# FiLM scale and shift on one core: small inputs first in 4 KB runs, accumulated matmuls, compute in program order

## The chip, the cores and the metric

One core of a Trainium2 chip runs the whole program. The metric is the device time of one execution in microseconds (us). A run is called slow when it takes over 1.5% more than the fastest of the same kernel; comparisons use the fast runs alone. Ratios compare the fast runs of two kernels in the same rounds, so they are not quite the ratio of the medians quoted. The span is the time that the profile covers; it is about 1.75 us shorter than the measured time.

## The reference

```python
# x [32, 512, 256], conditioning [32, 64], gamma_proj and beta_proj [64, 256], all float32
gamma = conditioning @ gamma_proj
beta = conditioning @ beta_proj
return (x * (1 + gamma[:, None, :]) + beta[:, None, :]).astype(np.float32)
```

Of the data, x comes in (16.78 MB) and the result goes out (16.78 MB). The three small inputs together are 0.14 MB.

## The kernel before

The batch is cut into four slabs of 8 samples; in a slab each of the 128 partitions holds 32 rows of 256 numbers. SyncE's queue loads x, ScalarE's queue loads the small inputs and later stores the result. TensorE makes gamma and beta for a slab, spread over the partitions. VectorE handles 11 of every 16 rows, straight from PSUM, and GpSimd handles the other 5, from a copy that ScalarE makes.

```python
nc.scalar.dma_start(out=cond_s, in_=conditioning)
gbproj = consts.tile([cond_dim, 2 * dim], f32)               # 64 partitions
nc.scalar.dma_start(out=gbproj[:, :dim], in_=gamma_proj)     # 1 KB runs
nc.scalar.dma_start(out=gbproj[:, dim:], in_=beta_proj)
# ... x: slab 0 in pieces of 8 and 24 rows, slabs 1 to 3 whole, all on nc.sync ...
nc.tensor.matmul(cond_T_p, lhsT=cond_s, rhs=rident, start=True, stop=True)
# ... copied to cond_T, then for each slab s:
nc.tensor.matmul(p_t, lhsT=cond_T[:, s * P : (s + 1) * P], rhs=gbproj, start=True, stop=True)
nc.scalar.activation(out=s_t[:, :dim], in_=p_t[:, :dim], ..., bias=1.0, scale=1.0)
nc.scalar.copy(out=s_t[:, dim:], in_=p_t[:, dim:])
# ... and for each half slab of 16 rows: v = 11 rows, w = 5 rows
nc.vector.scalar_tensor_tensor(out=v, in0=rows(g_p, nv), scalar=1.0, in1=v, op0=ALU.add, op1=ALU.mult)
nc.gpsimd.tensor_tensor(out=w, in0=w, in1=rows(g_s, nw), op=ALU.mult)
nc.vector.tensor_add(out=v, in0=v, in1=rows(b_p, nv))
nc.gpsimd.tensor_tensor(out=w, in0=w, in1=rows(b_s, nw), op=ALU.add)
nc.scalar.dma_start(out=o_v[s, :, r0 : r0 + GROUP, :], in_=xs[:, r0 : r0 + GROUP, :])
```

Of the kernel before, what the change touches and what calls it, by code (L numbers as in the profile page):

```python
# [2 lines left out]

# [5 lines left out]


@with_exitstack
def kernel(
    ctx: ExitStack,
    tc: tile.TileContext,
    x: bass.AP,
    conditioning: bass.AP,
    gamma_proj: bass.AP,
    beta_proj: bass.AP,
    out: bass.AP,  # L20
):
    nc = tc.nc
    f32 = mybir.dt.float32
    ALU = mybir.AluOpType

    batch, seq, dim = x.shape
    cond_dim = conditioning.shape[1]
    P = 128
    SLABS = 4
    BS = batch // SLABS  # L30
    REP = P // BS
    ROWS = BS * seq // P
    assert SLABS * BS == batch and REP * BS == P and ROWS * REP == seq

    x_v = x.flatten_outer_dims().rearrange("(s p r) d -> s p r d", s=SLABS, p=P)
    o_v = out.flatten_outer_dims().rearrange("(s p r) d -> s p r d", s=SLABS, p=P)

    LOADS = {0: [8, 24]}
    GROUP = 16
    ON_DVE = 11  # L40

    consts = ctx.enter_context(tc.tile_pool(name="consts", bufs=1))
    xpool = ctx.enter_context(tc.tile_pool(name="xpool", bufs=1))
    psum = ctx.enter_context(tc.tile_pool(name="psum", bufs=1, space=bass.MemoryType.PSUM))


    cond_s = consts.tile([batch, cond_dim], f32)
    nc.scalar.dma_start(out=cond_s, in_=conditioning)  # L48
    gbproj = consts.tile([cond_dim, 2 * dim], f32)
    nc.scalar.dma_start(out=gbproj[:, :dim], in_=gamma_proj)  # L50
    nc.scalar.dma_start(out=gbproj[:, dim:], in_=beta_proj)

    slabs = []
    for s in range(SLABS):
        xs = xpool.tile([P, ROWS, dim], f32, name=f"xs{s}")
        slabs.append(xs)
        r = 0
        for n in LOADS.get(s, [ROWS]):
            nc.sync.dma_start(out=xs[:, r : r + n, :], in_=x_v[s, :, r : r + n, :])
            r += n  # L60
        assert r == ROWS


    ident = consts.tile([batch, batch], f32)
    make_identity(nc, ident)
    rident = consts.tile([batch, batch * REP], f32)
    nc.vector.tensor_copy(  # L67
        out=rident.rearrange("p (b g) -> p b g", g=REP),
        in_=ident.to_broadcast([batch, batch, REP]),
    )  # L70
    cond_T_p = psum.tile([cond_dim, batch * REP], f32)
    nc.tensor.matmul(cond_T_p, lhsT=cond_s, rhs=rident, start=True, stop=True)  # L72
    cond_T = consts.tile([cond_dim, batch * REP], f32)
    nc.vector.tensor_copy(out=cond_T, in_=cond_T_p)  # L74

    gb_p, gb_s = [], []
    for s in range(SLABS):
        p_t = psum.tile([P, 2 * dim], f32, name=f"gb_p{s}")
        nc.tensor.matmul(p_t, lhsT=cond_T[:, s * P : (s + 1) * P], rhs=gbproj,  # L79
                         start=True, stop=True)  # L80
        s_t = consts.tile([P, 2 * dim], f32, name=f"gb_s{s}")
        nc.scalar.activation(out=s_t[:, :dim], in_=p_t[:, :dim],  # L82
                             func=mybir.ActivationFunctionType.Identity,
                             bias=1.0, scale=1.0)
        nc.scalar.copy(out=s_t[:, dim:], in_=p_t[:, dim:])  # L85
        gb_p.append(p_t)
        gb_s.append(s_t)

    def rows(t, n):
        return bass.AP(tensor=t.tensor, offset=t.offset, ap=[t.ap[0], [0, n], t.ap[1]])  # L90

    for s in range(SLABS):
        xs = slabs[s]
        g_p, b_p = gb_p[s][:, :dim], gb_p[s][:, dim:]
        g_s, b_s = gb_s[s][:, :dim], gb_s[s][:, dim:]
        for r0 in range(0, ROWS, GROUP):
            v = xs[:, r0 : r0 + ON_DVE, :]
            w = xs[:, r0 + ON_DVE : r0 + GROUP, :]
            nv, nw = ON_DVE, GROUP - ON_DVE
            nc.vector.scalar_tensor_tensor(out=v, in0=rows(g_p, nv), scalar=1.0, in1=v,  # L100
                                           op0=ALU.add, op1=ALU.mult)
            nc.gpsimd.tensor_tensor(out=w, in0=w, in1=rows(g_s, nw), op=ALU.mult)  # L102
            nc.vector.tensor_add(out=v, in0=v, in1=rows(b_p, nv))  # L103
            nc.gpsimd.tensor_tensor(out=w, in0=w, in1=rows(b_s, nw), op=ALU.add)  # L104
            nc.scalar.dma_start(out=o_v[s, :, r0 : r0 + GROUP, :],
                                in_=xs[:, r0 : r0 + GROUP, :])


# [1 line left out]
_INS = ['x', 'conditioning', 'gamma_proj', 'beta_proj']  # L110
_OUTS = [((32, 512, 256), 'float32')]


# [23 lines left out]
```

## Time and profile before

| | before |
|---|---|
| time, first three runs | 84.39, 85.98, 85.95 us (median 85.95, on which the prediction was made) |
| time, with three more runs beside the changed kernel | median 84.53 us, 84.39 to 85.98 (the four fast runs: 84.39 to 84.54) |
| span of the profiled run | 82.6 us |
| bytes moved | 33.69 MB |
| VectorE's first and last work on x | starts at 17.52, ends at 66.58 us |

### The profile page before, as it was taken

To read this page: it belongs to the slowest core of one execution; us is meant where nothing else is said; L and a number is where in the kernel's file an instruction comes from. 1 tells how busy PE (TensorE), PEld (TensorE's weight loads), DVE (VectorE), ACT (ScalarE), POOL (GpSimd) and SP (SyncE) were. 2 spreads that over 40 slices of the span, in tenths; PEclk is the share of its full clock that TensorE was granted. 3 is DMA by queue.
4 is the path that set the end of the run, shared out by engine and by line. 5 is a ranking of instruction groups with operands and counts; after the bars stand their busy time and mean duration, and the time that the engine had idled before them with its cause. 6 is when DMAs were issued, how large, how long until landed. Compare 5 with 4: busy or idle time off the path is not lost.

```text
span 82.6 us, 156 instructions
## 1 busy us (share of the span) xinstructions
PE 9.1 (11%) x10; PEld 2.8 (3%) x10; DVE 49.9 (60%) x18; ACT 3.9 (5%) x9; POOL 46.2 (56%) x22
## 2 busy tenths in 40 slices
PE   0080000899600000000000000000000000000000
PEld 0100000443000000000000000000000000000000
DVE  2011000059999999999999999999999920000000
ACT  0600000034400000000000000000000000000000
POOL 2000000069999999999999999999995000000000
DMA  3899999969969989998889979899999999999992
GB/s 56 337 508 397 389 397 524 460 302 508 508 270 492 508 381 381 413 476 381 381 381 556 460 302 460 381 468 421 429 452 389 468 421 421 460 389 452 437 421 87
DMA packets 2080, 33.69 MB, mean 408 GB/s; under 512 B 288, under 2 KB 416, under 8 KB 416
## 3 DMA queue, kind: packets, MB, share of 16 engines
q1 hardware_dynamic: 720, 16.78, 48.6%
q10 hardware_dynamic: 1360, 16.92, 48.0%
HBM read 16.92 MB, written 16.78 MB: 408 GB/s over the span
## 4 chain that ended last, share of the span: by engine, by line
DVE 49%; DMA 16%; issue 11%; PE 2%; ACTq 1%; ACT 1%
DVE xs L100 30%; DVE xs L103 19%; DMA gbproj<-in_beta_proj_dram 16%; PE gb_p L79 2%; ACTq L50 1%; ACTq L48 0%; ACT gb_s L82 0%; ACT gb_s L85 0%
## 5 line engine op out<-in xcount | busy, mean ns | idle before, releaser
L102 POOL TENSOR_TENSOR xs<-xs,gb_s 128x1280 f32<-128x1280 f32 x8 | 23.0, 2895 | 16.2 <-ACT gb_s L82 16.2
L100 DVE SCALAR_TENSOR_TENSOR xs<-gb_p,xs 128x2816 f32<-128x2816 f32 x8 | 24.7, 3083 | 10.9 <-ACT gb_s L85 10.9
L103 DVE TENSOR_TENSOR xs<-xs,gb_p 128x2816 f32<-128x2816 f32 x8 | 24.7, 3086 | 0.3
L104 POOL TENSOR_TENSOR xs<-xs,gb_s 128x1280 f32<-128x1280 f32 x8 | 23.0, 2893 | 0.0
L79 PE MATMUL gb_p<-gbproj,cond_T 64*128 64x512 f32 x8 | 7.2, 1074 | 8.9 <-DMA gbproj<-in_beta_proj_dram 8.9
L74 DVE COPY cond_T<-cond_T_p 64x512 f32<-64x512 f32 x1 | 0.7, 683 | 4.3 <-PE cond_T_p L72 4.3
L79 PEld LDWEIGHTS gb_p<-gbproj,cond_T 64*128 64x128 f32 x8 | 2.5, 328 | 13.7 <-issue 13.7
L72 PE MATMUL cond_T_p<-rident,cond_s 32*64 32x512 f32 x2 | 1.9, 1065 | 3.9 <-DMA cond_s<-in_conditioning_dram 3.9
L82 ACT ACTIVATE gb_s<-gb_p 128x256 f32<-128x256 f32 x4 | 1.5, 383 | 16.4 <-PE gb_p L79 16.4
L85 ACT COPY gb_s<-gb_p 128x256 f32<-128x256 f32 x4 | 1.5, 367 | 0.0
L82 ACT ACT_TABLE_LOAD x1 | 1.3, 1283 | 2.4 <-issue 2.4
L67 DVE COPY rident<-ident 32x512 f32<-32x512 f32 x1 | 0.4, 416 | 1.2 <-POOL ident masks.py:199 1.2
L72 PEld LDWEIGHTS cond_T_p<-rident,cond_s 32*64 32x64 f32 x2 | 0.3, 202 | 3.9 <-issue 3.9
masks.py:197 POOL MEMSET ident<- 32x32 f32 x1 | 0.1, 114 | 0.3 <-POOLq L121 0.3
masks.py:199 POOL TENSOR_SCALAR_AFFINE_SELECT ident<-ident 32x32 f32<-32x32 f32 x1 | 0.2, 202 | 0.1
L121 POOL MEMSET const-float32-0.0<- 128x1 f32 x1 | 0.1, 103 | 0.2 <-issue 0.2
L121 POOL MEMSET const-bfloat16-1.0<- 128x1 bf16 x1 | 0.1, 106 | 0.0
L121 POOL MEMSET const-uint8-127<- 128x1 uint8 x1 | 0.1, 106 | 0.0
L121 POOL MEMSET const-float32-1.0<- 128x1 f32 x1 | 0.1, 103 | 0.0
## 6 DMA issues: line engine op xcount, KB each, us to landing
out_dram<-xs ACTq DMA_DIRECT2D x8, 2048.0 KB, 18.2
xs<-in_x_dram SPq DMA_DIRECT2D x3, 4096.0 KB, 32.9
xs<-in_x_dram SPq DMA_DIRECT2D x1, 3072.0 KB, 12.2
xs<-in_x_dram SPq DMA_DIRECT2D x1, 1024.0 KB, 4.6
gbproj<-in_gamma_proj_dram ACTq DMA_DIRECT2D x1, 64.0 KB, 9.1
gbproj<-in_beta_proj_dram ACTq DMA_DIRECT2D x1, 64.0 KB, 12.9
cond_s<-in_conditioning_dram ACTq DMA_DIRECT2D x1, 8.0 KB, 3.0
```

What stands on the lines that cost most here:

```text
L50: nc.scalar.dma_start(out=gbproj[:, :dim], in_=gamma_proj)
L67: nc.vector.tensor_copy(out=rident.rearrange("p (b g) -> p b g", g=REP), in_=ident.to_broadcast([batch, batch, REP]),)
L72: nc.tensor.matmul(cond_T_p, lhsT=cond_s, rhs=rident, start=True, stop=True)
L74: nc.vector.tensor_copy(out=cond_T, in_=cond_T_p)
L79: nc.tensor.matmul(p_t, lhsT=cond_T[:, s * P : (s + 1) * P], rhs=gbproj, start=True, stop=True)
L82: nc.scalar.activation(out=s_t[:, :dim], in_=p_t[:, :dim], func=mybir.ActivationFunctionType.Identity, bias=1.0, scale=1.0)
L85: nc.scalar.copy(out=s_t[:, dim:], in_=p_t[:, dim:])
L100: nc.vector.scalar_tensor_tensor(out=v, in0=rows(g_p, nv), scalar=1.0, in1=v, op0=ALU.add, op1=ALU.mult)
L102: nc.gpsimd.tensor_tensor(out=w, in0=w, in1=rows(g_s, nw), op=ALU.mult)
L103: nc.vector.tensor_add(out=v, in0=v, in1=rows(b_p, nv))
L104: nc.gpsimd.tensor_tensor(out=w, in0=w, in1=rows(b_s, nw), op=ALU.add)
L121: nc = _bacc.Bacc("TRN2", target_bir_lowering=False, num_devices=1)
```

## The change

The intent is to start compute earlier. The projections come as 4 KB runs on 16 partitions, each as the first DMA of its queue, so that they land ahead of x. Sixteen partitions hold four rows each of the 64, so a product becomes four accumulated matmuls. The vector work is put in program order.

```diff
+    CP = 16
+    CJ = cond_dim // CP
     cond_s = consts.tile([batch, cond_dim], f32)
+    gproj = consts.tile([CP, CJ, dim], f32)
+    bproj = consts.tile([CP, CJ, dim], f32)
+    gproj_src = gamma_proj.rearrange("(q j) d -> q j d", j=CJ)
+    bproj_src = beta_proj.rearrange("(q j) d -> q j d", j=CJ)
+    nc.sync.dma_start(out=gproj, in_=gproj_src)
+    nc.scalar.dma_start(out=bproj, in_=bproj_src)
+    load(nc.sync, 0, 0)
     nc.scalar.dma_start(out=cond_s, in_=conditioning)
-    gbproj = consts.tile([cond_dim, 2 * dim], f32)
-    nc.scalar.dma_start(out=gbproj[:, :dim], in_=gamma_proj)
-    nc.scalar.dma_start(out=gbproj[:, dim:], in_=beta_proj)
+    load(nc.sync, 0, 1)
+    # ... slabs 1, 2, 3 on nc.sync
...
-        nc.tensor.matmul(p_t, lhsT=cond_T[:, s * P : (s + 1) * P], rhs=gbproj,
-                         start=True, stop=True)
+        # c_t: this slab's 8 columns of the transposed conditioning, spread over 128
+        for half, proj in ((p_t[:, :dim], gproj), (p_t[:, dim:], bproj)):
+            for j in range(CJ):
+                nc.tensor.matmul(half, lhsT=c_t[:, j, :], rhs=proj[:, j, :],
+                                 start=j == 0, stop=j == CJ - 1)
...
+    with tc.manual_schedule():        # the loop over slabs: instructions as written
```

More of the change, by code (lines that the diff above doesn't have):

```diff
@@ L28 @@
     P = 128
-    SLABS = 4
-    BS = batch // SLABS
-    REP = P // BS
-    ROWS = BS * seq // P
-    assert SLABS * BS == batch and REP * BS == P and ROWS * REP == seq
-    x_v = x.flatten_outer_dims().rearrange("(s p r) d -> s p r d", s=SLABS, p=P)
-    o_v = out.flatten_outer_dims().rearrange("(s p r) d -> s p r d", s=SLABS, p=P)
-    LOADS = {0: [8, 24]}
-    GROUP = 16
-    ON_DVE = 11
+    SLABS = [(8, [8, 24]), (8, [32]), (8, [32]), (8, [32])]
+    assert sum(n for n, _ in SLABS) == batch
+    STORES = [[16, 16], [16, 16], [16, 16], [16, 16]]
+    PIECE, ON_DVE = 16, 11
+    x_f = x.flatten_outer_dims()
+    o_f = out.flatten_outer_dims()
     consts = ctx.enter_context(tc.tile_pool(name="consts", bufs=1))
@@ L44 @@
     psum = ctx.enter_context(tc.tile_pool(name="psum", bufs=1, space=bass.MemoryType.PSUM))
-    cond_s = consts.tile([batch, cond_dim], f32)
-    nc.scalar.dma_start(out=cond_s, in_=conditioning)
-    gbproj = consts.tile([cond_dim, 2 * dim], f32)
-    nc.scalar.dma_start(out=gbproj[:, :dim], in_=gamma_proj)
-    nc.scalar.dma_start(out=gbproj[:, dim:], in_=beta_proj)
-    slabs = []
-    for s in range(SLABS):
-        xs = xpool.tile([P, ROWS, dim], f32, name=f"xs{s}")
-        slabs.append(xs)
-        r = 0
-        for n in LOADS.get(s, [ROWS]):
-            nc.sync.dma_start(out=xs[:, r : r + n, :], in_=x_v[s, :, r : r + n, :])
-            r += n
-        assert r == ROWS
+    slabs = []
@@ new lines, with load @@
+    b0 = 0
+    for s, (n, loads) in enumerate(SLABS):
+        assert P % n == 0
+        rows = n * seq // P
+        r0, r1 = b0 * seq, (b0 + n) * seq
+        slabs.append(dict(
+            n=n, b0=b0, rows=rows, loads=loads,
+            src=x_f[r0:r1, :].rearrange("(p r) d -> p r d", p=P),
+            dst=o_f[r0:r1, :].rearrange("(p r) d -> p r d", p=P),
+            xs=xpool.tile([P, rows, dim], f32, name=f"xs{s}"),
+        ))
+        b0 += n
+    def load(eng, s, i):
+        sl = slabs[s]
+        r = sum(sl["loads"][:i])
+        n = sl["loads"][i]
+        eng.dma_start(out=sl["xs"][:, r : r + n, :], in_=sl["src"][:, r : r + n, :])
@@ L64 @@
+    load(nc.sync, 1, 0)
+    load(nc.sync, 2, 0)
+    load(nc.sync, 3, 0)
     ident = consts.tile([batch, batch], f32)
     make_identity(nc, ident)
-    rident = consts.tile([batch, batch * REP], f32)
-    nc.vector.tensor_copy(
-        out=rident.rearrange("p (b g) -> p b g", g=REP),
-        in_=ident.to_broadcast([batch, batch, REP]),
-    )
-    cond_T_p = psum.tile([cond_dim, batch * REP], f32)
-    nc.tensor.matmul(cond_T_p, lhsT=cond_s, rhs=rident, start=True, stop=True)
-    cond_T = consts.tile([cond_dim, batch * REP], f32)
@@ L74 @@
-    nc.vector.tensor_copy(out=cond_T, in_=cond_T_p)
-    gb_p, gb_s = [], []
-    for s in range(SLABS):
+    gb_p, gb_s = [], []
+    cond_T_p = psum.tile([CP, CJ, batch], f32)
+    for j in range(CJ):
+        nc.tensor.matmul(cond_T_p[:, j, :],
+                         lhsT=cond_s.rearrange("b (q j) -> b j q", j=CJ)[:, j, :],
+                         rhs=ident, start=True, stop=True)
+    for s, sl in enumerate(slabs):
+        n, b0 = sl["n"], sl["b0"]
+        rep = P // n
+        c_t = consts.tile([CP, CJ, P], f32, name=f"cond_T{s}")
+        nc.vector.tensor_copy(
+            out=c_t.rearrange("q j (b g) -> q j b g", g=rep),
+            in_=cond_T_p[:, :, b0 : b0 + n].to_broadcast([CP, CJ, n, rep]),
+        )
@@ L78 @@
         p_t = psum.tile([P, 2 * dim], f32, name=f"gb_p{s}")
-        nc.tensor.matmul(p_t, lhsT=cond_T[:, s * P : (s + 1) * P], rhs=gbproj,
-                         start=True, stop=True)
+        for half, proj in ((p_t[:, :dim], gproj), (p_t[:, dim:], bproj)):
+            for j in range(CJ):
+                nc.tensor.matmul(half, lhsT=c_t[:, j, :], rhs=proj[:, j, :],
+                                 start=j == 0, stop=j == CJ - 1)
         s_t = consts.tile([P, 2 * dim], f32, name=f"gb_s{s}")
@@ L87, with spread @@
         gb_s.append(s_t)
-    def rows(t, n):
+    def spread(t, n):
         return bass.AP(tensor=t.tensor, offset=t.offset, ap=[t.ap[0], [0, n], t.ap[1]])
-    for s in range(SLABS):
-        xs = slabs[s]
-        g_p, b_p = gb_p[s][:, :dim], gb_p[s][:, dim:]
-        g_s, b_s = gb_s[s][:, :dim], gb_s[s][:, dim:]
-        for r0 in range(0, ROWS, GROUP):
-            v = xs[:, r0 : r0 + ON_DVE, :]
-            w = xs[:, r0 + ON_DVE : r0 + GROUP, :]
-            nv, nw = ON_DVE, GROUP - ON_DVE
-            nc.vector.scalar_tensor_tensor(out=v, in0=rows(g_p, nv), scalar=1.0, in1=v,
-                                           op0=ALU.add, op1=ALU.mult)
-            nc.gpsimd.tensor_tensor(out=w, in0=w, in1=rows(g_s, nw), op=ALU.mult)
-            nc.vector.tensor_add(out=v, in0=v, in1=rows(b_p, nv))
-            nc.gpsimd.tensor_tensor(out=w, in0=w, in1=rows(b_s, nw), op=ALU.add)
-            nc.scalar.dma_start(out=o_v[s, :, r0 : r0 + GROUP, :],
-                                in_=xs[:, r0 : r0 + GROUP, :])
+    with tc.manual_schedule():
+        for s, sl in enumerate(slabs):
+            xs = sl["xs"]
+            g_p, b_p = gb_p[s][:, :dim], gb_p[s][:, dim:]
+            g_s, b_s = gb_s[s][:, :dim], gb_s[s][:, dim:]
+            done = 0
+            for n in STORES[s]:
+                for q0 in range(done, done + n, PIECE):
+                    nv, nw = ON_DVE, PIECE - ON_DVE
+                    v = xs[:, q0 : q0 + nv, :]
+                    w = xs[:, q0 + nv : q0 + PIECE, :]
+                    nc.vector.scalar_tensor_tensor(out=v, in0=spread(g_p, nv), scalar=1.0, in1=v,
+                                                   op0=ALU.add, op1=ALU.mult)
+                    nc.gpsimd.tensor_tensor(out=w, in0=w, in1=spread(g_s, nw), op=ALU.mult)
+                    nc.vector.tensor_add(out=v, in0=v, in1=spread(b_p, nv))
+                    nc.gpsimd.tensor_tensor(out=w, in0=w, in1=spread(b_s, nw), op=ALU.add)
+                nc.scalar.dma_start(out=sl["dst"][:, done : done + n, :],
+                                    in_=xs[:, done : done + n, :])
+                done += n
+            assert done == sl["rows"]
 _INS = ['x', 'conditioning', 'gamma_proj', 'beta_proj']
```

## The prediction

> **What bounds the kernel now.** I read the page from the top, then the chain, then the table of stretches, and only then single instructions. First the slices of the span and the queues:
>
> ```profile
> DMA  3899999969969989998889979899999999999992
> ...
> DMA packets 2080, 33.69 MB, mean 408 GB/s; under 512 B 288, under 2 KB 416, under 8 KB 416
> ...
> q1 hardware_dynamic: 720, 16.78, 48.6%
> q10 hardware_dynamic: 1360, 16.92, 48.0%
> ```
>
> The reader is to see that the two queues add up to 96.6% of what the 16 DMA engines can give in 82.6 us. q1 holds the loads of x (16.78 MB), q10 the stores and the three small inputs. VectorE is busy for 60% and GpSimd for 56%. So the transfers are the first candidate, and there is 3.4% of the span, 2.8 us, in which the DMA engines do nothing.
>
> The chain that ended last seems to say something else:
>
> ```profile
> 1.72 12.90 DMA gbproj<-in_beta_proj_dram
> 14.62 0.14 issue
> 14.76 2.06 PE gb_p L79 x2
> ...
> 17.52 3.10 DVE xs L100
> ...
> 63.49 3.09 DVE xs L103
> ```
>
> It runs from the beta projection, which takes 12.9 us to land, over two matmuls and ScalarE to VectorE, which then never stops until 66.58. This is what the change attacks. But the chain follows instructions, and the last of them ends 16 us before the span does. Those 16 us, and what stands before them, are in the table by stretches (start:end, length, five engines, granted clock, DMA share, GB/s):
>
> ```profile
> 2.00:4.00 2.00, 0.08 (x1) 0.11 (x2) 0.00 (x0) 1.28 (x1) 0.00 (x0) 1.00 0.84 324
> 4.00:14.00 10.00, 1.85 (x2) 0.18 (x2) 0.68 (x1) 0.00 (x0) 0.00 (x0) 1.00 1.05 433
> 14.00:26.00 12.00, 7.16 (x8) 2.50 (x8) 8.45 (x3) 2.59 (x8) 8.70 (x4) 1.00 0.98 423
> ...
> 66.00:74.00 8.00, 0.00 (x0) 0.00 (x0) 0.58 (x1) 0.00 (x0) 0.00 (x0) 1.00 1.02 436
> 74.00:80.00 6.00, 0.00 (x0) 0.00 (x0) 0.00 (x0) 0.00 (x0) 0.00 (x0) 1.00 0.99 426
> 80.00:81.00 1.00, 0.00 (x0) 0.00 (x0) 0.00 (x0) 0.00 (x0) 0.00 (x0) 1.00 0.88 377
> ```
>
> From 4 to 80 us the share stays at 0.97 to 1.05 in every stretch, whether only loads run (433 and 423 GB/s), loads and stores mixed (414 to 451), or stores alone (436). While the projections are late, the loads of x use the time; after the last vector instruction a backlog of stores drains. The late start of compute is a wait that the DMA engines do not feel. My reading: the span is about 2 us to get going, 33.69 MB at about 427 GB/s (78.9 us), and 1.6 us after the last data. That sums to 82.5.
>
> **What the Trainium skill says.** (1) "DMA: Bandwidth & Descriptors", section "Where 436 GB/s comes from", gives 435 GB/s as the ceiling of the 16 engines. The trace agrees: 426 to 436 GB/s over the long stretches. (2) The same page, "Queues, rings and completion order", says that each engine takes turns between its queues packet by packet. The trace agrees: 64 KB of gamma took 9.1 us from issue to landing and beta 12.9, while x moved beside them. A projection of 64 rows gives each engine four 1 KB packets, each of which waits for a packet of x (8 KB, then 24 KB). (3) The same page, "Why a DMA increments its semaphore by 16 and not by 1", says that the slowest dimension sets how many engines a DMA uses, up to 16. Sixteen partitions should thus still use all 16, with one 4 KB packet each. The trace before has no 16-partition DMA to show it. (4) "TensorE: Matmul & The Clock Gate", "Step-by-step: what each phase is for", says that weights can be loaded behind a running matmul, and that the load's time goes by columns, not rows. The trace agrees on the first: loads of 334 ns started every 0.85 us, with no gap in the matmuls.
>
> **The change part by part.** *Small inputs.* Gamma goes first on SyncE's queue and beta first on ScalarE's, as 32 packets of 4 KB in place of 128 of 1 KB. Nothing long stands ahead of them; 128 KB at 427 GB/s is 0.3 us, so both should land by about 3.5 us (the 8 KB conditioning, first in line before, landed at 3.7). Conditioning is now second and issued 0.5 us later, with two packets per engine that take turns with 8 KB packets of x (about 0.3 us each): landing at about 4.5. The first x issue slips by the 0.4 us of gamma's issue, while some data is moving; I charge 0.1 us to the DMA engines and credit 0.1 us for the fewer packets.
>
> *Matmuls.* Before, a 512-column matmul is two instructions in the profile, paced at 0.853 us (weight loads at 15.75, 16.60, 17.45), so 1.7 us for a slab. After, a slab needs 8 matmuls of 256 columns, 16 instructions. At half of 0.853 they take 0.427 us each. But a weight load of 0.334 us began some 0.14 us after its predecessor's matmul, which gives 0.47 as the pace. I take 0.47: 16 x 0.47 = 7.5 us per slab, four times as long as before. The start is conditioning at 4.5, plus 0.7 for the four 32-column transposes, plus 0.7 for the copy that spreads a slab over 512 columns (683 ns before). So slab 0 runs from 5.9 to 13.4 and the others end at 20.9, 28.4 and 35.9. Add 0.7 us of ScalarE: first compute at about 14.1, against 17.5. The second piece of x's first slab landed at about 13.4, so it allows no more than this anyway. The gain on the chain is 3.4 us, not the 10 us by which beta lands earlier.
>
> *Compute.* The eight pairs of 3.08 and 3.09 us are unchanged: 49 us on VectorE. Four GpSimd instructions per slab stay at 2.9 us, now in the order multiply, add, multiply, add, so that the first half's GpSimd part is done after 5.8 us, not 8.6. VectorE thus ends at about 63.2, if x is there.
>
> *Stores.* Here the instruction order matters: on ScalarE's queue the first store stands after slab 2's copies, and the second after slab 3's. So they cannot be issued before 29.1 and 36.6, although their data is ready at 20.3 and 26.4. Before they went out at 25.9 and about 30. The later ones follow VectorE: about 36.9, 38.7, 44.8, 50.9, 57.0, 63.2.
>
> *Sum on the DMA engines.* Loads run alone from 2 to 29.1, at 426 GB/s: 11.5 MB. The remaining 5.2 MB share the engines with stores. A load packet is 32 KB and a store packet 16 KB, so taking turns gives loads two thirds, 284 GB/s: 18.4 us, which has x complete at 47.5. VectorE needs slab 3 at 50.9, so it does not starve. (The same arithmetic for before, from 25.9, gives 49.3; the traffic shows the last x data at about 49, and VectorE needed it at 54.25.) Stores have then moved 2.6 MB. 14.2 MB at 430 GB/s are 33 us more: 80.5, plus 1.6 is 82.1. No stretch has the engines idle, so what happens earlier is only another order of the same 33.69 MB. The span changes by a few tenths at most: **82.3 us predicted, against 82.6**.
>
> **The rivals.** *A: the chain bounds.* If the span ended with VectorE's work plus one fixed drain, 3.4 us would be gained: 79.2 us of span, 4% faster. Against it: 33.69 MB in 79.2 - 3.6 us would need 446 GB/s, more than any long stretch shows, and above the ceiling of 435. For it is only the chain's share of 16% for beta. I give 4% to this and anything else that is faster.
>
> *B: TensorE becomes the wait.* If weight loads were not hidden, an instruction would cost 0.427 + 0.334 = 0.76 us and a slab 12.2 us. The slabs would be ready at 18, 30, 42 and 54, the first store would leave at 43, the second at 55. The loads would be through at 41.4 alone, and the engines would idle for some 1.5 and then 7 us: about 91 us of span, 10% slower. Against it is the hidden loading in the trace before; for it, that the loads are now almost as long as the matmuls. By the same arithmetic the limit is about 0.62 us per instruction: below it the second store is issued before the DMA engines run dry.
>
> *C: earlier stores slow the loads, and VectorE starves on slab 3.* Even if the stores left at once, at 20.3, loads alone would bring 7.8 MB and the rest would take 31.7 us, to 52: 1 us late for VectorE, which would end at 64.5, with a backlog of stores still in front of it. It costs nothing either; the time stays at 82 to 83.
>
> **Range and chances.** A, B and C differ on the path, but only B breaks the DMA engines' continuity. The profiled run before had 82.6 us of span and 84.35 of time, 1.75 apart; 82.3 gives 84.1 as the time of a run of the quick kind. The three runs before were 84.39, 85.98 and 85.95: two levels, 1.6 us apart, of the same kernel, for which the profile gives no cause. The median may fall on either. I predict 85.1 us, between them, with 83.7 to 86.6 as the range for 8 in 10. Within 2%: 0.89. Slower: 0.07, most of it for B. Faster: 0.04, for A, or an unlucky mix of the two levels.
>
> **What would show it right or wrong.** Right: both projections land within 4 us; VectorE starts at 13.5 to 15 us, and ends at 62 to 65; the queues again add up to about 96% of the span; GB/s in the stretches from 4 to 80 us are within 3% of those before; the tail with stores alone is longer, by what VectorE ends earlier. The matmul step is wrong if slabs follow each other at other than 7 to 8 us; the order step, if the first store leaves well before 28 us. The whole is wrong if the DMA row has slices under 8 between 4 and 78 us (then B, and slower), or if the span falls below 81 us, which would mean that the engines had more to give than every stretch of the trace before shows.

## More of the kernel before

The two runs near 86 us are slow runs. The prediction shows the page's main lines. Beside them, two views matter later. The first is the page's groups of instructions of TensorE (line, engine, operation, names, shapes, count; busy us, mean ns of one; idle time before, and what ended it):

```profile
L79 PE MATMUL gb_p<-gbproj,cond_T 64*128 64x512 f32 x8 | 7.2, 1074 | 8.9 <-DMA gbproj<-in_beta_proj_dram 8.9
L79 PEld LDWEIGHTS gb_p<-gbproj,cond_T 64*128 64x128 f32 x8 | 2.5, 328 | 13.7 <-issue 13.7
```

All of gamma and beta take TensorE 7.2 us, and it waited 8.9 us for beta to land. The second is the timeline of ScalarE and its queue (start us, us, what):

```profile
22.24 0.37 ACT L85 COPY gb_s<-gb_p 128x256 f32<-128x256 f32 x1
25.94 41.06 ACTq L105 DMA_DIRECT2D out_dram<-xs  x8
```

ScalarE is done with its last copy before the first store is due, so no store waits for a copy. The first store leaves at 25.94 us.

## The result, and the profile after

The changed kernel takes 84.80 us at the median of 6 runs (84.66 to 84.96), against 84.53 us for the kernel before. The ratio of the fast runs is 1.004, with a 95% interval of 1.0022 to 1.0058: the same within 2%, and slower by a small amount that is clear of noise. No run of the changed kernel was slow, which six runs do not make a property of it: slow runs appeared later with the kernel before and with variants of the changed one.

First the page of the changed kernel, its DMA row over 40 slices, packets and queues:

```profile
DMA  1999999969997997999999799999999999999990
...
DMA packets 1985, 33.69 MB, mean 405 GB/s; under 512 B 289, under 2 KB 289, under 8 KB 321
...
q1 hardware_dynamic: 752, 16.84, 48.9%
q10 hardware_dynamic: 1232, 16.85, 47.4%
```

The queues again add up to 96.3% of 16 engines' time. Multiplied by the spans, that is 80.1 us of busy DMA engines after and 79.8 before (96.6% of 82.6). The small packets of 1 KB are gone, but the work of the engines has not shrunk.

Then the chain that ended last (start us, us, what):

```profile
1.19 4.80 DMA cond_s<-in_conditioning_dram
...
6.13 0.59 PE cond_T_p L88 x8
...
7.48 7.20 PE gb_p L102 x16
...
15.38 3.10 DVE xs L126
...
61.37 3.09 DVE xs L129
```

Conditioning, not beta, is the last input to land. It is followed by 7.2 us of matmuls for slab 0 alone, so compute starts at 15.38, which is 2.1 us earlier than before. It ends at 64.46, again 2.1 us earlier. The span is 0.6 us longer in these two profiled runs.

The table by stretches (start:end, length, busy time and count of PE, PEld, DVE, ACT and POOL, granted clock, DMA share, GB/s) shows where the 2.1 us went:

```profile
2.00:4.00 2.00, 0.00 (x0) 0.00 (x0) 0.00 (x0) 0.94 (x1) 0.00 (x0) 1.00 0.97 262
4.00:14.00 10.00, 7.10 (x23) 5.59 (x24) 2.47 (x4) 0.00 (x0) 0.00 (x0) 1.00 1.05 448
14.00:26.00 12.00, 12.00 (x30) 9.31 (x29) 10.55 (x4) 1.30 (x4) 10.68 (x4) 1.00 0.99 426
...
66.00:74.00 8.00, 0.00 (x0) 0.00 (x0) 0.00 (x0) 0.00 (x0) 0.00 (x0) 1.00 1.00 428
```

The DMA share is as full as before in every long stretch. The engines had no idle time to give to an earlier start; the end of the stores did not come earlier.

The groups of TensorE and the timeline of ScalarE's queue answer to those shown of before:

```profile
L102 PE MATMUL gb_p<-gproj,cond_T 16*128 16x256 f32 x32 | 14.6, 634 | 0.8 <-DVE cond_T L95 0.8
L102 PEld LDWEIGHTS gb_p<-gproj,cond_T 16*128 16x128 f32 x32 | 10.5, 330 | 3.8 <-DVE cond_T L95 0.9
```

```profile
28.35 0.38 ACT L105 ACTIVATE gb_s<-gb_p 128x256 f32<-128x256 f32 x1 [6.18 <-PE gb_p L102]
28.50 0.38 ACTq L131 DMA_DIRECT2D out_dram<-xs  x1
...
35.18 0.38 ACT L105 ACTIVATE gb_s<-gb_p 128x256 f32<-128x256 f32 x1 [6.18 <-PE gb_p L102]
35.27 0.37 ACTq L131 DMA_DIRECT2D out_dram<-xs  x1
```

The gamma half alone costs TensorE 14.6 us; the beta half adds 14.5. (The matmuls overlap, so 32 times the mean of 634 ns is more than 14.6 us.) From slab 1 on, ScalarE waits 6.18 us for each slab's gamma and beta. The first two stores stand behind the copies of slabs 2 and 3 in ScalarE's instruction stream, and leave at 28.50 and 35.27, later than the 25.94 of before, though compute began earlier.

### The profile page after: what moved, and what is told of

Read it like the earlier page. It is cut to its first block, busy times and chain, and to the rows that moved or that the text cites. A ratio compares the mean times of both kernels' runs of the same rounds, so it can differ in the third digit from the quotient of the medians.

```text
span 83.2 us, 282 instructions
## 1 busy us (share of the span) xinstructions
PE 28.2 (34%) x72; PEld 21.5 (26%) x72; DVE 51.3 (62%) x20; ACT 3.9 (5%) x9; POOL 46.6 (56%) x22
## 4 chain that ended last, share of the span: by engine, by line
DVE 49%; issue 11%; PE 9%; DMA 6%; ACT 1%; ACTq 1%
DVE xs L126 29%; DVE xs L129 19%; PE gb_p L102 9%; DMA cond_s<-in_conditioning_dram 6%; DVE cond_T L95 1%; PE cond_T_p L88 1%; ACTq L74 1%; ACT gb_s L105 0%; ACT gb_s L108 0%
## 5 line engine op out<-in xcount | busy, mean ns | idle before, releaser
L102 PE MATMUL gb_p<-gproj,cond_T 16*128 16x256 f32 x32 | 14.6, 634 | 0.8 <-DVE cond_T L95 0.8
L102 PE MATMUL gb_p<-bproj,cond_T 16*128 16x256 f32 x32 | 14.5, 629 | 0.0
L102 PEld LDWEIGHTS gb_p<-gproj,cond_T 16*128 16x128 f32 x32 | 10.5, 330 | 3.8 <-DVE cond_T L95 0.9
L102 PEld LDWEIGHTS gb_p<-bproj,cond_T 16*128 16x128 f32 x32 | 10.6, 332 | 3.0
L95 DVE COPY cond_T<-cond_T_p 16x512 f32<-16x512 f32 x4 | 2.5, 672 | 6.7 <-PE cond_T_p L88 6.7
L88 PE MATMUL cond_T_p<-ident,cond_s 32*16 32x32 f32 x8 | 0.6, 232 | 6.1 <-DMA cond_s<-in_conditioning_dram 6.1
```

Source lines behind the costliest of these rows:

```text
L88: nc.tensor.matmul(cond_T_p[:, j, :], lhsT=cond_s.rearrange("b (q j) -> b j q", j=CJ)[:, j, :], rhs=ident, start=True, stop=True)
L95: nc.vector.tensor_copy(out=c_t.rearrange("q j (b g) -> q j b g", g=rep), in_=cond_T_p[:, :, b0 : b0 + n].to_broadcast([CP, CJ, n, rep]),)
L102: nc.tensor.matmul(half, lhsT=c_t[:, j, :], rhs=proj[:, j, :], start=j == 0, stop=j == CJ - 1)
```

## The experiments

Twelve kernels ran. Unless said otherwise they are edits of the changed kernel, gave the right result, and their ratios are to the kernel before in the same rounds.

**All compute removed.**

```diff
-    # transposes, gamma and beta, copies
-    # scalar_tensor_tensor, tensor_add, tensor_tensor
     nc.scalar.dma_start(out=sl["dst"][:, done : done + n, :], in_=xs[:, done : done + n, :])
```

> The changed kernel with all compute taken out (wrong result on purpose): the same loads and stores on the same queues, each store waiting for its load alone, so stores start at about 14 us. Theory (the DMA engines bound the span from 4 to 80 us): 81.8 to 82.8 us of span, 83.5 to 84.6 us of time, within 1% of the kernel before, although no compute is left. Rival A (the chain through VectorE sets the end): without the 49 us of VectorE the span falls clearly, below 78 us. Rival (mixing reads and writes early costs bandwidth): above 84 us of span.

Measured: 84.86 us median, ratio 1.0053 (1.0013 to 1.0093), span 83.0 us: within the 1%, though just above the 83.5 to 84.6 us and 81.8 to 82.8 us expected. The result is wrong on purpose. Its page:

```profile
span 83.0 us, 64 instructions
...
DMA  1999989959999998999999899979999999999991
...
q1 hardware_dynamic: 752, 16.84, 48.9%
q10 hardware_dynamic: 1232, 16.85, 47.5%
```

With the matmuls, the copies and the 49 us of VectorE gone, and stores leaving from 13.43 us on, the time is the same. Only transfers are left, and they take 96.4% of 83.0 us, again 80.0 us. This is the floor of this set of DMAs, and the changed kernel (84.80 us) stands on it. It settles the main question: no start of compute, however early, could have shortened the changed kernel. The DMAs of the kernel before were not run bare; its 84.5 us lie within 0.5% of this floor.

**Compute delayed**, by 8.5 and 17 us as planned, by 6.6 and 15.3 us as measured. Idle matmuls stand ahead of slab 0's (five, or ten):

```diff
+    for i in range(5):                 # 10 in the second
+        nc.tensor.matmul(idle_p, lhsT=cond_s, rhs=wide, start=True, stop=True)
     for s, sl in enumerate(slabs):
```

> The changed kernel with five idle 512-column matmuls (10 instructions of 0.853 us, result unused) ahead of slab 0's matmuls: gamma and beta of every slab, and with them all compute and the first two stores, come 8.5 us later; VectorE starts at about 23.5 and the first store leaves at about 37. Theory (DMA engines bound): loads alone last until 41.5 us if no store comes, so the engines never idle; span 82.5 to 83.5 us, ratio 0.998 to 1.010. Rival A (the chain bounds): 8.5 us longer, 91 us, ratio 1.10.

> The same with ten idle matmuls, 17 us later: first store at about 44.4 us, second at about 51.2. Theory: the loads are through at about 41.5, so the DMA engines idle some 3 us before the first store and some 2 us after it: span about 87 us (86 to 88.5), ratio 1.04 to 1.065. Rival A: 17 us longer, 100 us, ratio 1.20.

| | first store leaves | VectorE ends | span | ratio (95%) | busy DMA (share x span) |
|---|---|---|---|---|---|
| changed kernel | 28.5 | 64.5 | 83.2 | 1.004 (1.0022 to 1.0058) | 80.1 |
| delayed by five | 35.1 | 71.1 | 83.5 | 1.0077 (1.0043 to 1.0111) | 80.0 |
| delayed by ten | 43.9 | 79.8 | 87.0 | 1.0514 (1.0489 to 1.054) | 79.3 |

The delay is less than planned, because conditioning landed sooner in these two runs (3.4 and 3.6 us after its issue, not 4.8) and the copy that spreads it ran beside the idle matmuls. VectorE ends 6.6 us later with five and nothing but 0.3 us comes of it; what these 0.3 us are is not settled. With ten, the loads run out before a store is there. The table by stretches of the second kernel:

```profile
40.00:42.00 2.00, 2.00 (x6) 1.55 (x5) 2.00 (x1) 0.00 (x0) 2.00 (x1) 1.00 0.61 262
42.00:44.00 2.00, 2.00 (x6) 1.53 (x6) 2.00 (x2) 0.28 (x1) 2.00 (x2) 1.00 0.00 0
...
50.00:52.00 2.00, 0.51 (x2) 0.00 (x0) 2.00 (x1) 0.65 (x2) 1.92 (x2) 1.00 0.30 131
```

The DMA share falls to 0 from 42 to 44 us and to 0.30 from 50 to 52, before the first and the second store. The busy time of the DMA engines stays at about 80 us, and the span is that plus the idle time. So the first 6.6 us of delay cost next to nothing, and the next 8.7 us cost 3.5 us: not the delay itself is paid, but the time in which the DMA engines then have nothing to carry (span less busy time is 3.5 us with five and 7.7 us with ten).

**TensorE's work doubled**, once with the changed kernel's program otherwise as it is (e7) and once with gamma and beta of slab s+2 placed after the stores of slab s (e8):

```diff
-    CP = 16
+    CP = 8          # 8 KB runs on 8 partitions, 16 matmuls of 256 columns per slab
```

> The changed kernel with the projections on 8 partitions in 8 KB runs, so 16 matmuls per slab in place of 8: 32 instructions of 0.427 us, 13.7 us per slab. Scalar order as in the changed kernel: first store held until slab 2's copies at about 48.6 us, second until slab 3's at 62.2. Theory: DMA engines idle from 41.5 to 48.6 and from about 53.5 to 62.2, then seven stores of 4.9 us: span about 98 us (96 to 100), ratio about 1.18. If the order on ScalarE did not hold the stores, it would be 82 to 85.

> The same doubled TensorE work with the interleaved program order of e3. The first stores leave at about 28 and 34 us. Theory: loads and stores fill the DMA engines until about 61 us, an idle of about 2 us may follow (slab 2's stores wait for slab 3's copies at about 63), span 82.5 to 85.5 us, ratio 1.00 to 1.03. If TensorE's time itself, and not the hold on the stores, was what cost in e7, the ratio stays above 1.10.

Measured: ratio 1.1538 (span 95.8 us) for e7, 1.0488 (span 86.8 us) for e8. Both numbers differ from what I expected, because I had misread the order of the instructions on ScalarE. In e7 the first three stores stand behind the copies of slabs 1, 2 and 3 and left at 37.07, 50.66 and 64.37, not from 48.6 on; in the changed kernel it is the first two, behind slabs 2 and 3, so e7 does not have the same order on ScalarE. In e8 the first two stand behind slab 1's copies and left at 36.94 and 37.43, not at 28 and 34. The cause is as expected. First stretches of e7, then one of e8:

```profile
48.00:52.00 4.00, 4.00 (x10) 3.10 (x10) 2.68 (x2) 0.65 (x2) 2.05 (x2) 1.00 0.16 70
...
56.00:64.00 8.00, 8.00 (x20) 5.86 (x18) 7.56 (x3) 0.00 (x0) 6.66 (x3) 1.00 0.00 0
```

```profile
62.00:66.00 4.00, 3.01 (x8) 1.81 (x6) 2.69 (x2) 0.65 (x2) 2.05 (x2) 1.00 0.08 33
```

e7 has two holes, one of them eight full microseconds in which the DMA engines carry nothing; e8 has one hole of about four. Busy DMA time is again 80.4 us (83.9% of 95.8) and 80.0 us (92.2% of 86.8). With the same matmuls, the order of the gamma and beta work and the stores is worth 9 us here.

**The stores let go in the changed kernel**, by the same interleaved order (e3), **x put first** (e2), **and both** (e4):

```diff
-    nc.sync.dma_start(out=gproj, in_=gproj_src)
-    nc.scalar.dma_start(out=bproj, in_=bproj_src)
     load(nc.sync, 0, 0)
     nc.scalar.dma_start(out=cond_s, in_=conditioning)
+    nc.scalar.dma_start(out=gproj, in_=gproj_src)
+    nc.scalar.dma_start(out=bproj, in_=bproj_src)
```

> The changed kernel, with the gamma and beta work of slab s+2 in program order after the stores of slab s, so that ScalarE's queue no longer holds the first two stores for the copies of slabs 2 and 3: they leave at about 21.7 and 27.8 us instead of 28.5 and 35.3. Theory (DMA engines bound, order of transfers is indifferent): 1.002 to 1.006 of the kernel before, as the changed kernel. Rival (held stores cost time): 0.985 to 0.998. x complete later, at about 52 us, and VectorE may wait up to 1 to 2 us on slab 3, at no cost.

> The changed kernel with the first load of x as the first DMA of the sync queue and conditioning, gamma, beta (still 4 KB runs) on the scalar queue. The changed kernel came out 0.4% slower than before (1.004). If that is the start of x's loads, 0.44 us later behind gamma's issue, it goes back to 0.998 to 1.001 of the kernel before. If it is the held stores or the longer work of TensorE, it stays at 1.003 to 1.006. Projections land some microseconds later than 3.4 us, compute starts within 14 to 17 us.

> Both edits, x first and the interleaved order. Theory: as e2, 0.998 to 1.001. If it beats every other version by over 0.5%, the order of the stores counts after all.

| | gamma first on SyncE's queue | x first |
|---|---|---|
| stores held by copies | 1.004 (changed kernel) | 0.9992 (0.9966 to 1.0019) |
| stores let go | 1.0039 (1.0006 to 1.0073) | 0.9993 (0.9966 to 1.002) |

The hold costs nothing: the first store left at 21.20 us in e3 in place of 28.50, without effect. The 0.4% goes with the order of the loads alone. The profiled run of e3 was a slow one, and of six runs each two of e2, three of e4 and two of e11 below were slow (86.4 to 88.2 us); what makes a run slow was not found.

**Which part of the order it is.** Two more orders of the same DMAs:

```diff
# e12: one swap on SyncE's queue          # e11: x first, and on ScalarE's queue beta, gamma, conditioning
-    nc.sync.dma_start(out=gproj, in_=gproj_src)
     load(nc.sync, 0, 0)
+    nc.sync.dma_start(out=gproj, in_=gproj_src)      # in e12 only
```

> As e2 (x first on the sync queue), but with the scalar queue in the order beta, gamma, conditioning, so conditioning is third and not first. If the 0.4% hangs on x being the first DMA of the sync queue: 0.997 to 1.001 of the kernel before. If it hangs on conditioning being first on the scalar queue: 1.003 to 1.006.

> The changed kernel with a single swap: on the sync queue gamma after the first piece of x, not before it; beta and conditioning on the scalar queue as changed. If it hangs on which DMA opens the sync queue: 0.997 to 1.001. If any projection ahead of the big loads of x costs the 0.4%, or if it is the scalar queue's order: 1.003 to 1.006.

Measured: 1.0001 (0.9978 to 1.0023) for e11, 1.0005 (0.999 to 1.002) for e12. A single swap, gamma behind the first piece of x in place of ahead of it, takes the 0.4% away (measured in other rounds than the 1.004, each against the kernel before), and of the orders tried on ScalarE's queue none mattered. The stretches at the start, of the changed kernel and then of e12, look as if they gave the reason:

```profile
2.00:2.50 0.50, 0.00 (x0) 0.00 (x0) 0.00 (x0) 0.50 (x1) 0.00 (x0) 1.00 2.02 344
2.50:3.00 0.50, 0.00 (x0) 0.00 (x0) 0.00 (x0) 0.45 (x1) 0.00 (x0) 1.00 0.12 16
```

```profile
2.00:2.50 0.50, 0.00 (x0) 0.00 (x0) 0.00 (x0) 0.50 (x1) 0.00 (x0) 1.00 0.57 131
2.50:3.00 0.50, 0.00 (x0) 0.00 (x0) 0.00 (x0) 0.42 (x1) 0.00 (x0) 1.00 0.58 197
```

In the changed kernel the projections are through by 2.5 us and hardly any of x has landed: 16 GB/s for half a microsecond. (A share above 1 counts packets whose time overlaps.) In e12 no such hole is there. But the hole is not the cost. The half microsecond before it makes up for it, and the same table over longer stretches shows no loss at the start: from 0 to 6 us both kernels moved 264 GB/s, and from 0 to 14 us the changed kernel moved more, 363 against 347. It falls behind later, from 14 to 60 us, with 422 against 430, at a DMA share of 1.00 in both; the kernel without compute, which also has gamma first, has 421 there. In these two profiled runs the time without work is about the same (83.2 less 80.1 is 3.1 us, 82.6 less 79.6 is 3.0); it is the packets that were busy longer in all. Why an order at the start should do that is open; the swap itself is what the runs show.

**x on both queues from the start**, with the small inputs on GpSimd's queue:

```diff
     load(nc.sync, 0, 0)
+    load(nc.scalar, 0, 1)
+    nc.gpsimd.dma_start(out=cond_s, in_=conditioning)     # then gproj and bproj
```

> The changed kernel with nothing ahead of x on either fast queue: the first piece of x's first slab is the first DMA of the sync queue, the second piece the first of the scalar queue, and conditioning, gamma and beta (4 KB runs) go on GpSimd's queue. In the changed kernel the DMA engines carry 16 GB/s from 2.5 to 3.0 us, a hole between the projections and x. Theory: filling the start is the only thing left to win, at most the 0.5 us that the engines run below 400 GB/s between 2 and 4 us: ratio 0.994 to 1.001. If a version that starts x on two queues is clearly under 0.994, the start held more than that.

Measured: 1.0048 (1.0031 to 1.0065), a miss. In its trace there is again a weak stretch, 197 GB/s from 3.0 to 3.5 us, and the small inputs took 6.8 to 11.7 us to land. Why it is slower was not followed up. Here x is first on both queues and 0.5% is lost all the same, so x first is not by itself enough; two queues for x are no way to a better start here.

**Program order alone**, in the kernel before:

```diff
-    for s in range(SLABS):
-        xs = slabs[s]
+    with tc.manual_schedule():
+        for s in range(SLABS):
+            xs = slabs[s]
```

> The kernel before with one part of the change alone: compute in program order, so that GpSimd does multiply, add, multiply, add. The first store leaves at about 23.8 us instead of 25.9. Theory: no effect, ratio 0.997 to 1.003. Rival (early stores are worth what they come earlier): 0.975.

Measured: 1.0009 (0.9978 to 1.0039). The first store left at 23.91 in place of 25.94, without effect.

No version beat the kernel before. After the copy without compute this was not to be hoped for from compute; only another order of the transfers could do it, and none of those tried did.

## Why the prediction was right or wrong, point by point

- **The bound was right.** Full DMA engines from 4 to 80 us were taken for the limit, and the chain for a wait that they do not feel. The copy without compute, at the same time, shows it directly. Rival A falls: the transfers had no room for the earlier start. Of the prediction's signs, these came as said: both projections landed by about 3.4 us, VectorE ended at 64.46, and the queues add up to 96.3%.
- **The time was right.** 84.80 us lies within 83.7 to 86.6. The 85.1 in the middle was a hedge between two levels of the kernel before; with more runs the slower level turned out to be the slow state, so that 84.80 lies near 85.1 is in part luck. The number to compare is the 84.1 foretold for a run of the quick kind: it is 0.7 us too low, more than the spread of the six runs (84.66 to 84.96).
- **The few tenths had the wrong sign.** The step "I charge 0.1 us to the DMA engines and credit 0.1 us for the fewer packets" failed. Putting gamma first cost 0.4% (1.004 against 1.0005 with the one swap), about 0.3 us, and fewer packets gave nothing that the busy time shows. The span came to 83.2 us (82.8 to 83.2 over six runs), not 82.3. The prediction's sum for after gave 82.1, and 82.3 was chosen above it; a sum good to some tenths cannot give the sign of 0.3 us.
- **The start of compute came late by 1.3 us**: 15.38 for 14.1. Conditioning landed at about 6.0 (4.80 us from its issue at 1.19), not 4.5; my reading, not tested, is that its packets took turns with those of x longer than I had allowed. The gain on the chain was thus 2.1 us, not 3.4, and the sign "VectorE starts at 13.5 to 15" failed. Nothing hung on it.
- **The matmul pace was 0.427 us, not 0.47.** Slabs follow each other 6.82 us apart (copies at 14.70, 21.53, 28.35), which is 16 times 0.427 and outside the 7 to 8 us of the sign. The weight loads were hidden completely; the 0.14 us between a matmul and the next load was not a floor. Rival B therefore did not occur.
- **Two signs were badly set.** The whole was to be wrong if the DMA row had slices under 8 between 4 and 78 us. The row after has four (6, 7, 7 and 7), and yet B did not occur: the row before, shown in the prediction, already has three (6, 6 and 7). GB/s was to stay within 3% in each stretch; it was 387 after 416 from 26 to 34 us and 410 after 451 from 50 to 54, while the shares stayed at 0.96 to 1.06. Nor is "426 to 436 GB/s over the long stretches" all of the trace before: it has 416 and 423 too. The share over long stretches, and the queues' sum, were the signs that held.
- **The order of the stores was right.** 28.5 and 35.3 for 29.1 and 36.6, behind the copies of slabs 2 and 3. Its harmlessness, which the sum on the DMA engines rests on, is shown by the interleaved kernel at the same time.
- **Rival B's mechanism was right in kind.** Where stores are held past the end of the loads, the time grows by the idle time of the DMA engines: 80 us busy in all the kernels from 83 to 96 us. My instruction orders for the two doubled kernels were wrong, though, and with them the expected figures.
- **Rival C did not occur in the changed kernel.** VectorE never waited for x after its start. In the interleaved kernel, where stores do leave early, VectorE waited 1.6 us for x (in the trace of a slow run), and the fast runs lost nothing, as C said.

## What to carry to other kernels

Before an engine's chain is shortened, multiply each queue's share by the span: if the DMA engines are busy all the time in every stretch, strip the compute and time the bare transfers, for that one run says what any compute change can be worth. Late compute or held stores cost next to nothing here until loads ran out before a store was ready, and then they cost the idle time of the DMA engines. The order of the first DMAs is worth a trial of its own: here a small one ahead of the bulk load cost 0.4%, for a reason that the traces leave open. And before a gap in one short stretch is called the cost, sum the bytes over a longer one.

## What the Trainium skill lacked or had wrong

- "DMA: Bandwidth & Descriptors", section "Issuing engines are not separate DMA queues", calls the sequencer's time to initiate a DMA usually small relative to the DMA. It lacks what a small DMA ahead of the bulk load can cost a transfer-bound kernel: one of 64 KB ahead of x on its queue cost 0.4% of 84.5 us (1.004 against 1.0005 with the two swapped). The first load of x was issued at 1.18 us in place of 0.74; that this time is the cost is not shown.
- The same page has no figure for how long a small DMA takes beside large packets. Gamma took 2.4 us from issue to landing as the first DMA of its queue, 5.6 us behind the first piece of x (e12), and 9.1 us in 1 KB runs as the second of its queue beside x (the kernel before); 8 KB of conditioning took 3.0 to 3.3 us as the first and 3.4 to 6.4 us as the second.
- "TensorE: Matmul & The Clock Gate", section "LDWEIGHTS (loading the stationary operand)", gives columns / 1.2 ns, an estimate of 107 ns for 128 columns. With float32, 128 columns took 330 ns here. That rows do not matter agrees (16 rows 330 ns, 64 rows 328). The page has no pace for float32 matmuls, and other pages only a count of passes and a peak rate; here a 256-column instruction followed the one before it after 0.427 us, and a product of float32 is two instructions (32 for 16 products of gamma).
